# Output weights prepared during the convolution, an in-place norm chain in PSUM, and dt steps spread over the u stage

## The chip, the cores and the metric

The kernel runs on one core of a Trainium2 chip. The metric is the device time of one execution in microseconds, taken as the median of several runs. Before the change the median of 3 runs is 1924.29 us (1920.41 to 1930.12).

## The reference

A layer of a diffusion backbone: 2048 latent tokens of width 1024, with a prefix of 256 context tokens. The tokens are normalised, modulated by `c`, projected once into five parts, and mixed in two ways: a Fourier group of 512 channels (a 2-D DFT, then a linear map, then a SiLU gate) and a state-space group of 1536 channels in 24 heads (a 3x3 depthwise convolution on x, B and C, a chunked scan in both directions, a gated RMSNorm). Both together go through one output projection of 2048 to 1024, are added to the input, and are normalised.

```python
def token_mixer(h, ...):
    u, zf, zs, xbc, dt_raw = jnp.split(h @ w_in, PROJ_SPLITS, axis=-1)
    four = fourier_mixer(u, zf, w_fourier, b_fourier)      # Re(fft2(u)) @ w_f + b_f, times silu(zf)
    xbc = depthwise_conv_grid(xbc, conv_w, conv_b, rows, cols)
    ssd, h_f, h_b = ssd_mixer(xbc, dt_raw, zs, dt_bias, a_log, d_skip, ssd_norm_w, h0_f, h0_b)
    return jnp.concatenate([four, ssd], axis=-1), h_f, h_b
...
    gated = y.reshape(bsz, length, g, r * p) * jax.nn.silu(zs.astype(f32)).reshape(bsz, length, g, r * p)
    gated = gated * lax.rsqrt(jnp.mean(gated * gated, axis=-1, keepdims=True) + EPS)
    out = gated.reshape(bsz, length, D_SSD).astype(zs.dtype) * norm_w
...
    x = x + gate[:, None] * (x_mix @ w_out[i])
return rmsnorm(x, final_norm_w)
```

## The kernel before

All large products are made of three matmuls. An fp32 operand is held as two parts of type fp32r, a high part (a copy with rounding) and a low part (the difference), and the product is high × high + high × low + low × high. `split` makes the parts: ACT copies (line 68), and DVE or POOL subtracts (line 72). Every DMA, load or store, goes through `load` (line 62) on one queue, that of SP; so it stands in one order with all others. A tile framework sets the semaphores and the order of instructions on each engine from the order of the code, from the buffers of each pool (a tile with `bufs=1` must be let go before the next one of its tag may be written), and from `tc.issue_after`, which puts a piece of code behind a given instruction.

The stages, by their time in the profiled execution:

- 0 to about 117 us: modulation, normalisation of x and context, the first projections (dt, parts of zf). The dt rows go to DRAM as `dtT_d`.
- about 117 to 267 us, the **u stage**: a loop over n2 from 0 to 15 (lines 502 to 525). Each step runs 24 matmuls (lines 509 to 511) for 128 tokens, splits the result into `uh` and `ul`, and, one step later, does the first DFT (`u_dft`, line 491), which is stored to `g_d`. Between these steps the dt work of the scan is put in, for three groups of six chunks: `dt_load` (after the steps 2, 6, 10) fetches 96x768 values in two DMAs into `ev` tiles, of which there are two buffers in all; `dt_soft` (steps 3, 7, 11) transposes them on PE (line 433) and computes the softplus in a chain on DVE and ACT (lines 435 to 447, 288 columns wide); `dt_cum` (5, 9, 13) makes the cumulative sums on PE (line 455) and exponentials; `dt_rows` (6, 10, 14) transposes the results back (line 480), splits them into `ev` tiles and stores them to `cum_d` and `q_d`. The steps are in the table `dt_work` (line 490). `ctx_block` at step 2 projects the context for dt and others.
- 267 to about 820 us, the **convolution**: 20 tiles of 128 channels (`conv_tile`). A tile loads its weights into a raw tile with one buffer, splits them, and projects in four blocks of 24 matmuls each into one of two PSUM banks (`pj`); ACT copies each block into an image `img`, which frees the bank. DVE then adds nine taps (`pacc`, line 624), ACT applies SiLU, PE transposes. B and C tiles are split into `sh` and `sl` (one buffer each, `hl_tiles`, line 580) and stored. `gate_step` (line 549) loads one piece of the modulation weights into an `ev` tile after each of the first 16 tiles.
- 820 to about 1130 us: zs projections and the backward scan.
- about 1130 to 1265 us, the **Fourier stage**: tables and second step, then `f_mm(dt, h, i)` (line 961) for four column blocks dt in the order 0, 3, 1, 2, two halves h and two parts i. `zf_load(dt)` (line 895) fetches the gate of a block (1 MB, two buffers), `f_gate` (line 944) multiplies on DVE and POOL, and after a block's second half the result is stored to `fm_d` (line 978). These pieces and the last zs projections are interleaved by given costs.
- 1265 to 1926 us, the **output loop**: 64 units u, of 16 chunks times 4 head groups, in a pipeline of steps s1 to s6 over successive units. `s1` loads decay rows (`rt`, `lt`, `cb`, `chl`) and makes the mask matrix `w` (matmul line 1081 into `parg`, DVE line 1083, ACT, DVE line 1086); `s2` loads, splits the state and runs `pyo` (line 1119); `s3` updates the state; `s4` computes y (`py`, lines 1155 and 1158), gates it (DVE line 1161) and sums its squares; `s5` makes the norm: a matmul with ones into `pn` (line 1171, a PSUM tile with one buffer), Ln, Exp and Square on ACT, then three DVE steps at lines 1177, 1178 and 1180, and the split of the normalised `gt` into `mh` and `ml`; `s6` multiplies by the output weights (lines 1214 to 1216).

The output weights are 16 blocks k of 128x1024 in fp32. Blocks of the state-space group are scaled by the norm weight `ssdw`. They live as high and low parts in `hl` and `hh`, the places of the activations, which become free late. `out_weights` (line 845) loads a block into a raw tile `wo` and splits it: for a scaled block ACT scales (line 858) and DVE scales and subtracts (line 859), for the four others ACT copies and POOL subtracts. Four blocks make the group of a head group g. Group 0 is done just before the rest of the Fourier stage's interleaved pieces; groups 1 to 3 (`out_group`, line 840) follow in the units 1 to 3 of the output loop, each block in two pieces.

Of the kernel before, what the change touches and what calls it, by code (L numbers as in the profile page):

```python
# [49 lines left out]
def mixer_layer(ctx: ExitStack, tc: tile.TileContext, A: dict, out: bass.AP, taps=None):  # L50
# [304 lines left out]
    with ExitStack() as pu:  # L355
# [62 lines left out]
        def dt_load(i):  # L418
            for q0 in range(0, NH, 4):
                nq = min(4, NH - q0)  # L420
                dtTs.append(evac_tile()[:2 * W2, :nq * P])
                load(dtTs[-1], dtT_d[:, (NH * i + q0) * P:(NH * i + q0 + nq) * P])

        def dt_soft(i):
# [4 lines left out]
            for q0 in range(0, NH, 4):  # L429
                nq = min(4, NH - q0)  # L430
                dtT = dtTs.pop(0)
                for q in range(nq):
                    mm(dview(pt)[:, :, q0 + q], dtT[:, q * P:(q + 1) * P], D0["i2"], start=True, stop=True)
# [56 lines left out]
        dt_work = {3 + 4 * i + q: (fn, i) for i in range(3) for q, fn in ((0, dt_soft), (2, dt_cum), (3, dt_rows))}  # L490
# [11 lines left out]
        for n2 in range(16):  # L502
            if n2 == 2:
                ctx_block()
            po = main_psum()
            for k in range(KT):
                a = hh[:, k].rearrange("p (a b) -> p b a", b=16)[:, n2]
                b = hl[:, k].rearrange("p (a b) -> p b a", b=16)[:, n2]
                mm(po, a, wuh[:, k], start=(k == 0), stop=False)
# [20 lines left out]
    gate = gatep.tile([P, D], F32, name="gate")  # L530

    with ExitStack() as pc_:
# [73 lines left out]

        cso = {}
# [81 lines left out]
    ssdw = const_tile("ssdw", hfp)  # L689
# [148 lines left out]
    wcols = [1536, 512, 0, 1024]  # L838

    def out_group(g):  # L840
        with tc.issue_after(fo["st"]), tc.issue_after(units[g]["ld"]), tc.issue_after(units[g]["exp"]):
            for n in range(4 * g, 4 * g + 4):
                out_weights(n, lambda sh: wk.tile(sh, F32, name="wo", tag="xr"), 2)

    def out_weights(n, raw_tile, parts):
        k = worder[n]
        r, c = 2 * (n % 4), wcols[n // 4]
        wos[k] = tuple(t[:, r:r + 2, c:c + 512] for t in (hl, hh))
        for q in range(parts):
            m = 2 // parts  # L850
            hi, lo = (t[:, m * q:m * q + m] for t in wos[k])
            raw = raw_tile([P, m, 512])
            load(raw, A["wout"][k].rearrange("p (a b) -> p a b", a=2)[:, m * q:m * q + m])
            if k < 4:
                split(hi, lo, raw, nc.gpsimd)
            else:
                sc_ = ssdw[:, k - 4:k - 3]
                nc.scalar.activation(hi, raw, AF.Copy, scale=sc_)  # L858
                nc.vector.scalar_tensor_tensor(out=lo, in0=raw, scalar=sc_, in1=hi.bitcast(F32),  # L859
                                               op0=ALU.mult, op1=ALU.subtract)  # L860
# [180 lines left out]
    for n in range(4):  # L1041
        out_weights(n, lambda sh: W["p"].tile(sh, F32, name="wo", tag="raw", bufs=1), 1)
# [6 lines left out]
    for n in range(4, 4):  # L1049
        out_weights(n, lambda sh: W["p"].tile(sh, F32, name="wo", tag="raw", bufs=1), 1)  # L1050
# [117 lines left out]
    def s5(u):  # L1168
# [8 lines left out]
        nc.vector.scalar_tensor_tensor(out=tt, in0=pn, scalar=EPS * GW, in1=tt, op0=ALU.add, op1=ALU.mult)  # L1177
        nc.vector.scalar_tensor_tensor(out=rs, in0=tt, scalar=1.5, in1=rs, op0=ALU.subtract, op1=ALU.mult)
        mx = d["gt"]
        nc.vector.tensor_tensor(out=mx, in0=mx, in1=rs[:].unsqueeze(1).broadcast_to([P, 3, P]), op=ALU.mult)  # L1180
# [71 lines left out]
    for u in range(NU + 2):  # L1252
# [4 lines left out]
        if 0 < u < G:  # L1257
            out_group(u)
# [117 lines left out]
```

## Time and profile before

| | before |
|---|---|
| median of 3 runs | 1924.29 us |
| the profiled execution's own time | 1927.71 us |
| span of the profiled execution | 1925.9 us |
| PE busy | 1824.7 us |
| DVE busy | 1325.2 us |
| ACT busy | 854.5 us |
| POOL busy | 887.0 us |
| DMA, bytes moved | 268.22 MB |

The profile shows one execution. PE, DVE, ACT and POOL are the matrix, vector, activation and general engines, and SPq is the queue of SyncE, which issues the DMAs. "Busy" counts the time of an engine's instructions; PEclk is the clock granted to PE, 1.00 or tenths at full speed. A windows row gives start and end, length, busy time and count of each engine, then PEclk, the mean busy share of the DMA engines and what they moved. A row of a group shows line, engine, operation, output<-inputs, shapes, count, busy time in us, mean ns of one, then the idle time of the engine before these instructions and what ended it. A row of the waits says which engine, tile and line waited for which other, for how long in total, how often and how long at most. A row of the timeline gives start and length in us, and in brackets the idle time before it. A row with three durations gives the least, the median and the greatest in ns, then the first and the last start in us.

### The profile page before, as it was taken

The page shows a single profiled execution, that of the slowest core. Times are in us where ns is not written, and L with a number is a line of the kernel's source. Part 1 is how long each engine was busy: PE and PEld are TensorE (multiplying, and loading weights), DVE is VectorE, ACT ScalarE, POOL GpSimd, SP SyncE. Part 2 cuts the span into 40 slices and gives each one's busy share as a digit, 9 for nine tenths or more (in the row PEclk, how much of TensorE's full clock was granted, in tenths as well). Part 3 has the DMA queues.
Part 4 walks back from the last instruction along what each step waited for, and adds up shares of the span by engine and source line. Part 5 has one row for each costly group of instructions (what it writes and reads, how often), then busy time and mean ns, then how long its engine had stood idle before and what let it go on. Part 6 is the DMA issues. An engine that isn't in the chain of part 4 may idle for free.

```text
span 1925.9 us, 27805 instructions
## 1 busy us (share of the span) xinstructions
PE 1824.7 (95%) x9142; PEld 1501.7 (78%) x9142; DVE 1325.2 (69%) x1830; ACT 854.5 (44%) x1940; POOL 887.0 (46%) x766
## 2 busy tenths in 40 slices
PE   6998899999999999989999999978999999999997
PEld 2787787888888888878888877856777777777775
DVE  3744359888888888748666631478786887688874
ACT  3632114444345344336666653435443444344442
POOL 1321012213123022059777732267766776677742
PEclk9998899999999999999999999979999999999998
DMA  7332243323233233367777774656443444444441
GB/s 272 146 97 80 64 121 111 102 82 94 79 100 103 66 91 99 103 203 214 216 211 213 213 252 152 199 176 185 148 148 117 132 136 135 130 130 135 142 137 39
DMA packets 273169, 268.22 MB, mean 139 GB/s; under 512 B 32545, under 2 KB 240801, under 8 KB 272514
## 3 DMA queue, kind: packets, MB, share of 16 engines
q1 hardware_dynamic: 273026, 266.45, 45.8%
q8 instruction: 73, 1.20, 0.3%
q14 instruction: 70, 0.57, 0.1%
HBM read 180.05 MB, written 86.32 MB: 138 GB/s over the span
## 4 chain that ended last, share of the span: by engine, by line
PE 69%; DVE 6%; DMA 5%; issue 2%; POOL 2%; ACT 1%; SPq 0%; DVEq 0%; ACTq 0%; POOLq 0%
PE pj L177 12%; PE pj L176 12%; PE pj L175 12%; PE po L1216 5%; PE po L1214 5%; PE po L1215 5%; PE py L1155 2%; PE ptr L569 2%; PE parg L1081 2%; PE py L1158 1%; DMA wo<-in_wout 1%; DMA xg<-xtok_d 1%; DVE pacc L624 1%; PE ptr L599 1%; PE ptr L808 1%
## 5 line engine op out<-in xcount | busy, mean ns | idle before, releaser
L177 PE MATMUL pj<-hh,wl 128*128 128x512 f32 x1152 | 452.3, 393 | 1.0 <-POOL wl L72 1.0
L624 DVE SCALAR_TENSOR_TENSOR pacc<-img,c_convw,pacc 128x1024 f32<-128x1024 f32 x320 | 409.8, 1287 | 61.0 <-ACT pacc L621 52.4
L175 PE MATMUL pj<-hh,wh 128*128 128x512 f32 x1152 | 449.3, 394 | 2.5 <-ACT img L68 2.5
L176 PE MATMUL pj<-hl,wh 128*128 128x512 f32 x1152 | 451.5, 392 | 0.0
L72 POOL TENSOR_TENSOR wl<-raw,wh 128x1024 fp32r<-128x1024 f32 x48 | 115.9, 2416 | 476.4 <-ACT wh L68 470.9
L177 PEld LDWEIGHTS pj<-hh,wl 128*128 128x128 f32 x1152 | 216.3, 188 | 47.3 <-POOL wl L72 1.6
L175 PEld LDWEIGHTS pj<-hh,wh 128*128 128x128 f32 x1152 | 216.7, 188 | 43.4 <-ACT img L68 2.7
L176 PEld LDWEIGHTS pj<-hl,wh 128*128 128x128 f32 x1152 | 216.4, 188 | 40.9 <-issue 1.8
L1214 PE MATMUL po<-hl,mh 128*128 128x512 f32 x384 | 158.2, 412 | 2.8 <-ACT hl L858 1.7
L1215 PE MATMUL po<-hh,mh 128*128 128x512 f32 x384 | 154.9, 403 | 1.4 <-DVE hh L859 1.4
L1216 PE MATMUL po<-hl,ml 128*128 128x512 f32 x384 | 149.4, 407 | 5.7 <-POOL ml L72 5.6
L794 ACT ACTIVATE xd<-xt,smb 128x64 f32<-128x64 f32 x384 | 100.8, 336 | 81.4 <-POOL yb L798 79.5
L68 ACT ACTIVATE img<-pj 128x512 f32<-128x512 f32 x80 | 47.6, 594 | 152.7 <-PE pj L177 152.7
L1085 ACT ACTIVATE w<-parg 128x384 f32<-128x384 f32 x128 | 62.2, 486 | 109.7 <-DVE parg L1083 109.4
L72 DVE TENSOR_TENSOR xl<-xw,xh 128x384 fp32r<-128x384 f32 x76 | 65.2, 862 | 55.0 <-ACT xh L68 54.0
L1081 PE MATMUL parg<-rt,lt 128*128 128x384 f32 x256 | 89.7, 376 | 7.5 <-DVE parg L1083 6.5
L1083 DVE COPY_PREDICATED parg<-msk,parg 128x384 f32<-128x384 uint8 x128 | 70.8, 553 | 35.5 <-PE parg L1081 35.2
L1124 POOL TENSOR_TENSOR ts<-ts,yb 128x384 f32<-128x384 f32 x64 | 72.3, 1130 | 48.9 <-issue 25.0
L72 POOL TENSOR_TENSOR ml<-gt,mh 128x384 fp32r<-128x384 f32 x64 | 69.9, 1092 | 54.0 <-ACT mh L68 49.2
L1086 DVE TENSOR_TENSOR w<-w,cb 128x768 f32<-128x768 f32 x64 | 84.6, 1322 | 14.6 <-ACT w L1085 13.8
L68 ACT ACTIVATE xh<-xw 128x384 fp32r<-128x384 f32 x136 | 69.7, 515 | 49.1 <-POOL xw L1135 22.0
L72 DVE TENSOR_TENSOR sl<-hbk,sh 128x384 fp32r<-128x384 f32 x64 | 64.3, 1005 | 37.3 <-ACT sh L68 37.1
(377 smaller groups left out, 4057.5 us busy)
## 6 DMA issues: line engine op xcount, KB each, us to landing
raw<-in_win SPq DMA_DIRECT2D x48, 512.0 KB
xt<-xtok_d SPq DMA_DIRECT2D x80, 192.0 KB
xtok_d<-tk SPq DMA_DIRECT2D x48, 256.0 KB
zsT_d<-ev SPq DMA_DIRECT2D x48, 256.0 KB
yb_d<-yb SPq DMA_DIRECT2D x64, 192.0 KB
yb<-yb_d SPq DMA_DIRECT2D x64, 192.0 KB
zs<-zsT_d SPq DMA_DIRECT2D x64, 192.0 KB
xg<-xtok_d SPq DMA_DIRECT2D x64, 192.0 KB
```

The source lines that it names most:

```text
L68: return nc.scalar.activation(dst, src, AF.Copy).ins
L72: (lo_engine or nc.vector).tensor_tensor(out=lo, in0=src, in1=hi.bitcast(F32), op=ALU.subtract)
L175: mm(po, wh[:, k], a, start=(k == 0), stop=False)
L176: mm(po, wh[:, k], b, start=False, stop=False)
L177: done["mm"] = mm(po, wl[:, k], a, start=False, stop=(k == KT - 1)).ins
L624: nc.vector.scalar_tensor_tensor(out=acc, in0=im[:, r0 + dy:r0 + dy + 16, dx:dx + GRID_W], scalar=tap(t), in1=acc, op0=ALU.mult, op1=ALU.add)
L794: nc.scalar.activation(xd[:, h], d["x"][:, h], AF.Copy, scale=smb[:, 3, c, g * HG + h:g * HG + h + 1])
L1081: mm(po, l[:, dr], r[:, cols], start=True, stop=True)
L1086: nc.vector.tensor_tensor(out=w, in0=w, in1=cb[:].unsqueeze(1).broadcast_to([P, HG, P]), op=ALU.mult)
L1214: mm(po, a, wh[:, i], start=(g == 0 and q == 0), stop=False)
L1215: mm(po, a, wl[:, i], start=False, stop=False)
L1216: mm(po, b, wh[:, i], start=False, stop=(g == 3 and q == 3))
```

## The change

**Output weights.** A new DRAM scratch `wo_d` holds all 16 blocks as high and low parts. After each of the 20 convolution tiles one or two of 32 pieces are made (`wout_piece`): load of 128x512 into an `ev` tile, for the 12 scaled blocks ACT scales it in place, ACT copies it to `sh`, POOL subtracts into `sl`, and both are stored to `wo_d`. `out_weights` and `out_group` are gone; `w_load` only fetches both parts of a block, 512 KB each, into places of `hl` and `hh` that are given by the table `wplace`. Group 0 is fetched before the rest of the Fourier pieces, group 1 among these pieces ahead of the last two pairs of `f_mm`, groups 2 and 3 in the first two steps of the output loop, behind the last store to `fm_d` and the loads of the next unit. The `f_mm` order within the last two blocks becomes (1,0), (2,0), (1,1), (2,1), so that places in `hl` come free sooner.

**dt steps.** A group's dt rows are loaded by one DMA into the raw weight tile instead of two `ev` tiles, after the steps 1, 4 and 9. Softplus runs in steps 2, 7, 12, sums in 5, 10, 14, rows in 6, 11, 15. `ctx_block` moves to step 1.

**Norm chain.** The results of lines 1177 and 1178 are written to `pn` in PSUM in place, and line 1180 reads it there.

```diff
+        def wout_piece(n):
+            k, h = divmod(n, 2)
+            cs = slice(512 * h, 512 * h + 512)
+            raw = evac_tile()
+            load(raw, A["wout"][k][:, cs])
+            if k >= 4:
+                nc.scalar.activation(raw, raw, AF.Copy, scale=ssdw[:, k - 4:k - 3])
+            parts = [t[:].rearrange("p a b -> p (a b)") for t in hl_tiles()]
+            split(*parts, raw, nc.gpsimd)
+            for i in range(2):
+                store(wo_d[k, :, i, cs].bitcast(F32), parts[i].bitcast(F32))
...
             if n < 2 * KT:
                 gate_step(*divmod(n, KT))
+            for q in range(32 * n // 20, 32 * (n + 1) // 20):
+                wout_piece(q)
...
-            for q0 in range(0, NH, 4):
-                nq = min(4, NH - q0)
-                dtTs.append(evac_tile()[:2 * W2, :nq * P])
-                load(dtTs[-1], dtT_d[:, (NH * i + q0) * P:(NH * i + q0 + nq) * P])
+            raw = W["p"].tile([P, 2, 512], F32, name="rawu", tag="raw", bufs=1)
+            dtTs.append(raw[:].rearrange("p a b -> p (a b)")[:2 * W2, :NH * P])
+            load(dtTs[-1], dtT_d[:, NH * P * i:NH * P * (i + 1)])
...
-        dt_work = {3 + 4 * i + q: (fn, i) for i in range(3) for q, fn in ((0, dt_soft), (2, dt_cum), (3, dt_rows))}
+        dt_work = {2 + 5 * i + q: (fn, i) for i in range(3) for q, fn in ((0, dt_soft), (3, dt_cum), (4, dt_rows))}
+        dt_work[14], dt_work[15] = (dt_cum, 2), (dt_rows, 2)
...
-            if n2 in (2, 6, 10):
+            if n2 in (1, 4, 9):
                 dt_load(n2 // 4)
...
+    wplace = [((hl, 1536), (hh, 1536)), ((hl, 0), (hl, 1024)), ((hl, 512), (hh, 1024)), ((hh, 0), (hh, 512))]
+
+    def w_load(n):
+        r, k = 2 * (n % 4), worder[n]
+        wos[k] = tuple(t[:, r:r + 2, c:c + 512] for t, c in wplace[n // 4])
+        for i in range(2):
+            load(wos[k][i].bitcast(F32), wo_d[k, :, i].rearrange("p (a b) -> p a b", a=2).bitcast(F32))
...
+    fmm = [(dt, h) for dt in dts[:2] for h in range(2)] + [(dt, h) for h in range(2) for dt in dts[2:]]
+    for n, (dt, h) in enumerate(fmm):
+        if n in (4, 5):
             side.append((0.0, zf_load(dt)))
+        if n == 6:
+            side.append((0.0, lambda: w_group(1)))
+        side += [(2.6, f_mm(dt, h, i)) for i in range(2)]
...
-        nc.vector.scalar_tensor_tensor(out=tt, in0=pn, scalar=EPS * GW, in1=tt, op0=ALU.add, op1=ALU.mult)
-        nc.vector.scalar_tensor_tensor(out=rs, in0=tt, scalar=1.5, in1=rs, op0=ALU.subtract, op1=ALU.mult)
+        nc.vector.scalar_tensor_tensor(out=pn, in0=pn, scalar=EPS * GW, in1=tt, op0=ALU.add, op1=ALU.mult)
+        nc.vector.scalar_tensor_tensor(out=pn, in0=pn, scalar=1.5, in1=rs, op0=ALU.subtract, op1=ALU.mult)
         mx = d["gt"]
-        nc.vector.tensor_tensor(out=mx, in0=mx, in1=rs[:].unsqueeze(1).broadcast_to([P, 3, P]), op=ALU.mult)
+        nc.vector.tensor_tensor(out=mx, in0=mx, in1=pn[:].unsqueeze(1).broadcast_to([P, 3, P]), op=ALU.mult)
...
-        if 0 < u < G:
-            out_group(u)
+        if u < 2:
+            with tc.issue_after(fo["st"]), tc.issue_after(units[u + 1]["ld"]):
+                w_group(u + 2)
```

The order of SP's DMAs in the u stage, before, around the load for the second dt group (`cum_d` and `q_d` are the stores of the row step before it, `g_d` those of the DFT):

```order
L63 DMA cum_d<-ev 48x512 x2
L63 DMA g_d<-gs 128x4x128
L63 DMA cum_d<-ev 48x256 x2
L63 DMA q_d<-ev 48x512 x2
L63 DMA q_d<-ev 48x256 x2
L63 DMA ev<-dtT_d 96x512
L63 DMA g_d<-gs 128x4x128
L63 DMA ev<-dtT_d 96x256
```

And now, where the loads for the first two groups stand (`rawv` is the context's raw tile, `smb_d` a store of the first sums):

```order
L63 DMA rawv<-in_ctx 128x1024
L63 DMA rawu<-dtT_d 96x768
L63 DMA g_d<-gs 128x4x128
L63 DMA rawu<-dtT_d 96x768
L63 DMA g_d<-gs 128x4x128
L63 DMA dtT_d<-ev 96x256
L63 DMA g_d<-gs 128x4x128
L63 DMA smb_d<-wl 128x144
```

The second group's load stood behind the stores of the first group's rows; it now stands ahead of the first group's sums.

The order of SP's DMAs at the end of the Fourier stage, before (`wo<-in_wout` is a block of group 0, `chl`, `lt` and `rt` are loads of the first units):

```order
L63 DMA zsT_d<-ev 128x4x128
L63 DMA fm_d<-zf 128x16x128
L63 DMA wo<-in_wout 128x1024
L63 DMA zf<-zfT_d 128x2048
L63 DMA fm_d<-zf 128x16x128 x2
L63 DMA chl<-chl_d 128x256 x2
L63 DMA lt_11007<-q_d 6x128
L63 DMA rt_11005<-cum_d 2x6x128
```

And now (the first row is group 1, the pairs after `fm_d` are group 2):

```order
L63 DMA hl<-wo_d 128x2x512 x8
L63 DMA zf<-zfT_d 128x2048
L63 DMA fm_d<-zf 128x16x128 x2
L63 DMA hl<-wo_d 128x2x512
L63 DMA hh<-wo_d 128x2x512
L63 DMA hl<-wo_d 128x2x512
L63 DMA hh<-wo_d 128x2x512
L63 DMA hl<-wo_d 128x2x512
L63 DMA hh<-wo_d 128x2x512
L63 DMA hl<-wo_d 128x2x512
L63 DMA hh<-wo_d 128x2x512
L63 DMA rt_11280<-cum_d 2x6x128
```

Eight loads of 512 KB now stand ahead of the last load of zf, and eight more between the last store of `fm_d` and the third unit's first load.

The order on ACT in the first convolution tile, before (`img` is the image that frees a PSUM bank, `wh` the weights' high part):

```order
L68 ACTIVATE ev<-pj 48x512
L68 ACTIVATE wh<-raw 128x1024
L68 ACTIVATE ev<-pj 48x512
L68 ACTIVATE uh<-pj 128x512
L68 ACTIVATE img_2048<-pj 128x8x64 x2
L621 ACTIVATE pacc<-img_2048,c_convw 128x1024
```

And now:

```order
L68 ACTIVATE ev<-pj 48x512
L68 ACTIVATE wh<-raw 128x1024
L68 ACTIVATE ev<-pj 48x512
L68 ACTIVATE sh<-ev 128x512
L68 ACTIVATE img_2045<-pj 128x8x64 x2
L633 ACTIVATE pacc<-img_2045,c_convw 128x1024
```

The first piece's copy into `sh` now stands ahead of the first two copies into `img`.

More of the change, by code (lines that the diff above doesn't have):

```diff
@@ L92, in mixer_layer @@
     yb_d = scratch("yb_d", [NCH, P, DS])
+    wo_d = scratch("wo_d", [16, P, 2, D], F32R)
     fm_d = scratch("fm_d", [NCH, P, 4, P])
@@ L428, in dt_soft @@
             pt = dt_psum()
[L429 to L433, printed above, removed]
+            dtT = dtTs.pop()
+            for q in range(NH):
+                mm(dview(pt)[:, :, q], dtT[:, q * P:(q + 1) * P], D0["i2"], start=True, stop=True)
             v, e, u, s1_, dtt = (D0[t] for t in ("v", "e", "u", "s1", "dtt"))
@@ L502, in mixer_layer @@
         for n2 in range(16):
-            if n2 == 2:
+            if n2 == 1:
                 ctx_block()
@@ L530, in mixer_layer @@
     gate = gatep.tile([P, D], F32, name="gate")
+    ssdw = const_tile("ssdw", gatep)
     with ExitStack() as pc_:
@@ L688, in mixer_layer @@
     hf = hfp.tile([P, DS], F32, name="hf")
-    ssdw = const_tile("ssdw", hfp)
     pp_ = ctx.enter_context(ExitStack())
@@ L837, in mixer_layer, with w_group @@
     worder = [k for g in range(G) for k in (4 + 3 * g, 5 + 3 * g, 6 + 3 * g, g)]
[L838 to L860, printed above, removed]
+    wplace = [((hl, 1536), (hh, 1536)), ((hl, 0), (hl, 1024)), ((hl, 512), (hh, 1024)), ((hh, 0), (hh, 512))]
[4 more added lines that the diff above has]
+            load(wos[k][i].bitcast(F32), wo_d[k, :, i].rearrange("p (a b) -> p a b", a=2).bitcast(F32))
+    def w_group(g):
+        for n in range(4 * g, 4 * g + 4):
+            w_load(n)
     pfb = ctx.enter_context(ExitStack())
@@ L1015, in mixer_layer @@
     side.append((0.0, f_switch))
-    tail = []
-    for n, dt in enumerate(dts):
-        if n > 1:
+    fmm = [(dt, h) for dt in dts[:2] for h in range(2)] + [(dt, h) for h in range(2) for dt in dts[2:]]
+    for n, (dt, h) in enumerate(fmm):
+        if n in (4, 5):
             side.append((0.0, zf_load(dt)))
-        for h in range(2):
-            for i in range(2):
-                (tail if 2 * n + h >= 8 else side).append((2.6, f_mm(dt, h, i)))
+        if n == 6:
+            side.append((0.0, lambda: w_group(1)))
+        side += [(2.6, f_mm(dt, h, i)) for i in range(2)]
     left = interleave(zs_ops([(i, (3,)) for i in range(19, 7, -1)]), side, 10, .75)
@@ L1039, in mixer_layer @@
         nc.vector.tensor_copy(out=t, in_=st2[:, :2])
-    for n in range(4):
-        out_weights(n, lambda sh: W["p"].tile(sh, F32, name="wo", tag="raw", bufs=1), 1)
+    w_group(0)
     for _, fn in left:
@@ L1048, in mixer_layer @@
     pre2 = preload(LNEXP)
-    for n in range(4, 4):
-        out_weights(n, lambda sh: W["p"].tile(sh, F32, name="wo", tag="raw", bufs=1), 1)
     units = {}
@@ L1090, in mixer_layer @@
         s1(u)
-        for _, fn in tail[len(tail) // 2 * u:len(tail) // 2 * (u + 1)]:
-            fn()
     pfb.close()
```

## The prediction

> **What bounds the kernel now.** I read the page first, then the windows by stage, then PE's waits, then groups and timeline rows. The page:
>
> ```profile
> span 1925.9 us, 27805 instructions
> PE 1824.7 (95%) x9142; PEld 1501.7 (78%) x9142; DVE 1325.2 (69%) x1830; ACT 854.5 (44%) x1940; POOL 887.0 (46%) x766
> PE   6998899999999999989999999978999999999997
> PEclk9998899999999999999999999979999999999998
> ```
>
> PE is busy 95% of the span; time can only come out of its idle slices and of slices where the clock dips. Apart from the two ends, they are slices 4 and 5 (the u stage) and 27 and 28 (start of the output loop), and the change touches both. The windows, in us:
>
> ```profile
> core 0: us, PE busy (x) PEld busy (x) DVE busy (x) ACT busy (x) POOL busy (x), PEclk, DMA share, GB/s
> 0.00:50.00 50.00, 31.78 (x137) 13.73 (x138) 16.67 (x37) 15.81 (x31) 7.96 (x8) 1.00 0.78 278
> 150.00:160.00 10.00, 7.35 (x28) 6.21 (x28) 1.39 (x3) 1.32 (x2) 3.07 (x2) 0.83 0.54 160
> 170.00:180.00 10.00, 7.34 (x21) 6.20 (x22) 4.55 (x11) 1.68 (x4) 0.00 (x0) 0.66 0.35 78
> 190.00:200.00 10.00, 5.04 (x18) 4.12 (x17) 1.61 (x3) 0.86 (x2) 0.00 (x0) 0.78 0.29 80
> 200.00:210.00 10.00, 10.00 (x41) 9.24 (x41) 5.13 (x9) 1.49 (x3) 0.00 (x0) 0.88 0.09 26
> 230.00:240.00 10.00, 7.55 (x31) 6.88 (x32) 0.93 (x3) 0.00 (x0) 0.00 (x0) 0.83 0.22 59
> 267.00:820.00 553.00, 550.49 (x2810) 467.85 (x2809) 463.80 (x390) 235.43 (x361) 115.65 (x74) 1.00 0.33 95
> 1265.00:1360.00 95.00, 72.92 (x353) 54.03 (x352) 75.43 (x114) 48.69 (x107) 71.31 (x66) 0.84 0.60 183
> 1400.00:1880.00 480.00, 460.05 (x2525) 367.45 (x2524) 373.72 (x631) 211.38 (x543) 335.91 (x309) 0.99 0.44 134
> ```
>
> The convolution (267:820) has 2.5 us of idle PE: nothing to win there, only to lose. The steady output loop (1400:1880) has 480 − 460.05 = 20 us idle in 480. Its first 95 us run 353 matmuls, where the steady rate of 2525 / 480 = 5.26 per us would need 67 us: some 28 us are lost.
>
> **Part 1, the dt steps in the u stage.** PE's waits between 117 and 267 us (total, times, longest), and five rows of the timeline, the last two the start and end of a softplus chain on DVE:
>
> ```profile
> PE pj L433 <- DMA ev<-dtT_d: 11.6, 3, 5.0
> PE pj L455 <- DVE wh L447: 5.1, 2, 3.2
> ```
>
> ```profile
> 153.43 1.09 PE L433 MATMUL pj<-wh,ev 96*128 96x48 f32 x8 [2.21 <-DMA ev<-dtT_d]
> 192.96 0.30 SPq L63 DMA_DIRECT2D ev<-dtT_d  x1
> 195.69 1.91 PE L433 MATMUL pj<-wh,ev 96*128 96x48 f32 x8 [4.96 <-DMA ev<-dtT_d]
> 203.61 0.46 DVE L435 TENSOR_TENSOR wh<-pj,wh 128x288 f32<-128x288 f32 x1 [10.23 <-PE pj L433]
> 211.98 0.46 DVE L447 TENSOR_TENSOR wh<-wl,wh 128x288 f32<-128x288 f32 x1
> ```
>
> The load for the second softplus leaves only at 192.96, because its `ev` buffers are held by the stores of the row step in front of it; its first matmul starts at 195.69 after 4.96 us of idle PE. Afterwards the load has a tile of its own and leaves three steps of n2 ahead of its use for the second and third group (n2 4 for 7, 9 for 12), and no store of a row step holds its buffer. A step is 24 matmuls, about 6 us (200:210 ran 41 in 10 us), so 18 us of lead stand against 2.7 us from issue to first use: those waits go. For the first group the distance is still one step (n2 1 for 2), so its 2.21 us stay. The cumulative sums wait 5.1 us for the softplus chain on DVE; they move from two steps behind it to three (two for the third group), and the chain takes 212.44 − 203.61 = 8.8 us, less than two steps once nothing holds up its start: gone. Idle removed: 11.6 + 5.1 − 2.2 = 14.5 us. The clock: behind each gap the windows grant less than 1; (1 − clock) × 10 us is 1.7, 3.4, 2.2, 1.2 and 1.7 in the five windows. The first stays, the others make 8.5, of which I strike 0.5 for half clock on an idle PE. **Part 1: −22.5 us**; bounds −14 (the clock dips anyway) and −26 (the first wait goes too, with its dip).
>
> **Part 2, the output weights split during the convolution.** Added there: 32 pieces of 128x512, after each of 20 convolution tiles one or two. Each is one load and two stores of 256 KB, for 24 of them a scaling on ACT, for all a copy on ACT and a subtraction on POOL. Prices from rows of the same shape:
>
> ```profile
> L858 ACT ACTIVATE hl<-wo,c_ssdw 128x512 fp32r<-128x512 f32 x18 | 12.9, 719 | 9.5 <-DMA wo<-in_wout 9.3
> L68 ACT ACTIVATE sh<-so 128x512 fp32r<-128x512 f32 x16 | 10.1, 633 | 7.7 <-DMA chl_d<-sh 6.9
> L72 POOL TENSOR_TENSOR sl<-so,sh 128x512 fp32r<-128x512 f32 x16 | 20.7, 1296 | 59.3 <-ACT sh L68 39.5 <-DMA chl_d<-sl 19.8
> PE pj L175 <- ACT img L68: 2.5, 1, 2.5
> ```
>
> ACT: 24 × 0.719 + 32 × 0.633 = 37.5 us onto 235 of 553. POOL: 32 × 1.296 = 41.5 onto 116. DMA: 96 transfers, 25.2 MB onto 95 GB/s × 553 us = 52.5 MB, to some 140 GB/s, half of the 278 that 0:50 shows at a share of 0.78. PE stays the bound, so the work itself costs nothing. What can cost is ACT's order: the copy into `sh` waits for the piece's load and for the stores out of the single `sh`, and behind it on ACT stand the copies into `img` that free PE's two PSUM banks. A block is 24 matmuls, again about 6 us, so ACT may stand still some 5 us before PE stops. In the row of sh<-so above 6.9 us of ACT's idle time ended on a store out of `sh` over 16 copies, 0.4 us each; and one such stop shows on PE, of 2.5 us. Two such stops: **+5 us**, bounds 0 and +10 (four). Below 0 nothing, since only 2.5 us are idle there.
>
> **Part 3, the start of the output loop.** Removed from 1217 to 1349 us are 28 loads of `wo` and their splits:
>
> ```profile
> L63 SPq DMA_DIRECT2D wo<-in_wout x28: 332/356/528, 1217.4 to 1349.0; - x28
> L858 ACT ACTIVATE hl<-wo,c_ssdw x21: 706/722/1155, 1230.6 to 1346.6; 128x512 fp32r<-128x512 f32 x18, 128x1024 fp32r<-128x1024 f32 x3
> L859 DVE SCALAR_TENSOR_TENSOR hh<-wo,c_ssdw,hl x21: 741/1023/1566, 1232.2 to 1347.4; 128x512 fp32r<-128x512 f32 x18, 128x1024 fp32r<-128x1024 f32 x3
> PE py L1155 <- DVE w L1086: 5.9, 5, 2.0
> PE pyo L1119 <- DMA chl<-chl_d: 4.4, 4, 3.4
> PE pyo L1119 <- DVE yy L950: 3.2, 1, 3.2
> PE po L1214 <- ACT hl L858: 1.7, 1, 1.7
> PE po L1215 <- DVE hh L859: 1.4, 3, 0.6
> ```
>
> DVE loses 21 × about 1.06 = 22 us and ACT 21 × about 0.78 = 16. The last five rows are PE's largest waits there: only 1.7 + 1.4 us are for the split itself, 9.1 for DVE (`w`, `yy`) and 4.4 for a load. A lighter DVE could win those 9.1, the direct 3.1, and the dips behind them: (1 − 0.84) × 95 = 15 us are lost to the clock. So at best about −15, taking half of the 28.
>
> Against it stand the bytes. A group of weights is now 4 × 2 loads of 512 KB, 4.19 MB, twice what it was. At 278 / 0.78 = 356 GB/s a group takes 11.8 us on all DMA engines. SP issues the eight of group 1 behind fm_d of dt 3, and only then the load of zf for dt 2 and the last two fm_d; then eight of group 2, then the second unit's small loads, and group 3 behind those. Two rows on the zf of dt 2 now:
>
> ```profile
> 1253.54 0.33 SPq L63 DMA_DIRECT2D zf<-zfT_d  x1
> 1261.16 9.95 SPq L63 DMA_DIRECT2D fm_d<-zf  x2
> ```
>
> Were it 11.8 us later, the gates of dt 1 and 2 on DVE and POOL, and the first pyo behind them on PE, begin about 11 us later. Unit 2's loads come another 11.8 us behind group 2, of which the backlog of 18 of the first 24 output matmuls that PE runs ahead of unit 2 (about 4 us) and the late gates cover a part; group 3 comes half under cover. So three groups are 35 us of queue on the way, of which I leave 12 to 13 uncovered, against −15 of work gone: **−2 us**, bounds −15 (the queue is hidden) and +15 (most of it shows).
>
> [...]
>
> **Part 4, the norm chain in place in PSUM.**
>
> ```profile
> L1180 DVE TENSOR_TENSOR gt<-gt,rs 128x384 f32<-128x384 f32 x64 | 53.6, 838 | 1.2
> L1178 DVE SCALAR_TENSOR_TENSOR rs<-tt,rs 128x128 f32<-128x128 f32 x64 | 32.1, 502 | 1.4
> L1177 DVE SCALAR_TENSOR_TENSOR tt<-pn,tt 128x128 f32<-128x128 f32 x64 | 18.2, 285 | 21.4 <-ACT tt L1176 20.9
> L1161 DVE SCALAR_TENSOR_TENSOR gt<-py,zs 128x384 f32<-128x384 f32 x64 | 35.3, 551 | 26.0 <-PE py L1158 14.1 <-POOL xw L1135 5.7 <-issue 3.4
> ```
>
> L1177 reads one operand from PSUM and takes 285 ns where L1178 with the same size reads two from SBUF and takes 502; L1161 with one operand in PSUM takes 551 where L1180 with both in SBUF takes 838. Afterwards L1178 and L1180 each have an operand in PSUM: 64 × (502 − 285) = 13.9 and 64 × (838 − 551) = 18.4, together 32.3 us of DVE, 0.5 us a unit. PE is idle 20 of 480 us in the steady loop, some for DVE; I take a quarter of that, **−5 us**; bounds −15 and +4, since the one `pn` bank is now held until L1180 instead of L1177, and the next unit's norm matmul may wait for it.
>
> [...]
>
> **The sum.** −22.5 + 5 − 2 − 5 = −24.5 us on the profiled execution's 1927.7 us (its span and 1.8 around it), which is 3.4 above the median of 1924.3. The median comes to 1899.8, so **1900**.
>
> **The rivals.**
> (a) *The queue shows at the start of the output loop*: part 3 at +10 to +15 and the rest as forecast: 1912 to 1917, about 1915. For it: eight half-megabyte loads stand in front of zf and of unit 2. Against it: PE has other work queued, and the DMA share there is 0.60. Chance 0.20.
> (b) *Everything comes in*: part 3 at −15, part 4 at −10, part 2 at 0: about 1877, between 1868 and 1888. For it: DVE and ACT lose 38 us exactly where PE waits for DVE. Chance 0.15.
> (c) *The dt change doesn't do what it says*: the chain on DVE stays as long, PE now reaches the sums sooner, and waits of the same size move to them; part 1 gives −4 instead of −22.5: 1918. For it: DVE began 203.61 − 195.69 = 8 us after the first matmul of its step. Against it: the added step of distance. Chance 0.10.
> (d) *Slower*: ACT stops at the pieces. A piece's copy sits on ACT until its load has come and the stores of the piece before have left `sh`; if that keeps the `img` copies back by 1.5 us beyond PE's two banks in each of 32 pieces, part 2 costs 48 and the time is 1900 + 43 = 1943. It decides where ACT stands more than 5 us at a time; the 6.9 us in 16 copies speak against it, the doubled traffic for it. Part 2 must reach 39 of those 48 us to bring the time past 1933.9. Chance 0.10.
> The forecast itself, 1888 to 1912, has 0.45.
>
> **How the numbers follow.** 0.5%, or 9.6 us, is about what a measurement of this kernel can tell from no change: faster means under 1914.7, slower over 1933.9. Faster: forecast 0.45, (b) 0.15, half of (a) 0.10: 0.70, less 0.02 for its tails, 0.68. Same: the other half of (a) 0.10, (c) 0.10: 0.20. Slower: (d) and the tails, 0.12. The range runs from inside (b), 1874, through (a) and (c) to 1926, the sum with parts 2 and 3 at their dear ends (1922) and a little; it leaves out (d) and the low part of (b).
>
> **What would show it.** Part 1: PE's wait for the dt load 2 us instead of 11.6, that for L447 under 1, and a clock of 1.0 in all windows of the u stage but one or two. Part 2: PE idle under 13 us from 267 to 820, with `img` on ACT named as releaser. Part 3: the first units' norm matmuls come within a few us of where they were, counted from the end of the convolution; PE's waits name loads rather than DVE. Part 4: L1178 near 285 ns, L1180 near 550. I am wrong if the convolution is longer by over 10 us, if L1180 stays at 838, or if the first 95 us of the output loop lose more than 45.

## The result, and the profile after

| | before | after |
|---|---|---|
| median of 5 runs | 1924.29 us | 1913.20 us |
| the profiled execution's own time | 1927.71 us | 1912.61 us |
| its span | 1925.9 us | 1910.8 us |

The changed kernel takes 0.9937 of the time before, with a 95% interval of 0.9915 to 0.9958: 11.1 us less in the medians, 15.1 in the two spans. The prediction was 1900 us, a gain of 24.3. Faster was right, the size was less than half. The page after:

```profile
span 1910.8 us, 28132 instructions
PE 1809.4 (95%) x9142; PEld 1492.4 (78%) x9142; DVE 1258.5 (66%) x1809; ACT 873.9 (46%) x1968; POOL 906.2 (47%) x791
PE   6989999999999999989999999957999999999997
PEclk8999999999999999999999999977999999999999
```

The hole in slices 4 and 5 is gone. The one in slices 27 and 28 is still there, and deeper (5, where the lowest digit was 7). The same in windows; the start of the output loop, which was 1265 to 1360, now lies at 1250 to 1345:

```profile
core 0: us, PE busy (x) PEld busy (x) DVE busy (x) ACT busy (x) POOL busy (x), PEclk, DMA share, GB/s
150.00:160.00 10.00, 9.77 (x49) 9.36 (x48) 7.03 (x12) 1.87 (x4) 0.12 (x1) 1.00 0.33 93
170.00:180.00 10.00, 10.00 (x52) 9.54 (x52) 3.55 (x8) 2.86 (x6) 0.00 (x0) 1.00 0.34 72
190.00:200.00 10.00, 10.00 (x44) 9.84 (x44) 6.91 (x13) 1.80 (x4) 0.00 (x0) 1.00 0.30 86
200.00:210.00 10.00, 10.00 (x46) 9.67 (x45) 4.05 (x8) 2.38 (x5) 0.00 (x0) 1.00 0.18 43
230.00:240.00 10.00, 10.00 (x45) 9.78 (x45) 6.93 (x13) 2.35 (x5) 1.07 (x1) 1.00 0.46 130
245.00:795.00 550.00, 544.51 (x2773) 460.39 (x2772) 462.74 (x391) 268.43 (x416) 162.80 (x109) 1.00 0.45 140
1250.00:1345.00 95.00, 59.19 (x281) 46.11 (x280) 43.55 (x76) 26.55 (x63) 46.99 (x46) 0.75 0.73 238
1400.00:1880.00 480.00, 465.49 (x2590) 373.23 (x2589) 349.51 (x640) 215.15 (x548) 331.01 (x313) 1.00 0.44 133
```

DVE and ACT have less to do there (43.6 and 26.6 us, from 75.4 and 48.7), partly because fewer units get through: PE does 281 matmuls in 95 us, where it did 353.

A table by stage puts every kernel on one scale. Each number is the distance between two rows of the timeline in that kernel's profiled execution: the first matmul of the u stage, the first of the convolution, the end of the last SiLU of a convolution tile, the start of the last three Fourier matmuls, the norm matmul of unit 8, that of unit 63. "Scan and Fourier" joins everything from that SiLU to those matmuls. In the first three columns, kernels with the same code in a stage differ by up to 4 us or so. In the last two they differ by more, because the mark at unit 8 can move by 7 us while the sum of the two columns hardly changes; a table behind the experiments has that sum.

| us in the stage | u stage | convolution | scan and Fourier | output start, to unit 8 | units 8 to 63 |
|---|---|---|---|---|---|
| before | 149.9 | 542.6 | 454.2 | 114.9 | 527.0 |
| after | 126.2 | 549.6 | 454.9 | 125.2 | 515.8 |
| difference | −23.7 | +7.0 | +0.7 | +10.3 | −11.2 |
| forecast | −22.5 | +5 | 0 | −2 | −5, over all units |

Together −16.9; the rest of the 15.1 is 1.7 us in front of the u stage. Three terms are near their forecast or better, one is wrong in sign: the start of the output loop. These are PE's largest waits there (total, times, longest; `issue` names no other engine):

```profile
PE pyo L1115 <- DVE yy L951: 16.5, 1, 16.5
PE parg L1079 <- DMA rt<-cum_d: 4.1, 1, 4.1
PE pyo L1115 <- DMA chl<-chl_d: 3.6, 3, 1.9
PE pn L1167 <- DVE s L1161: 3.1, 2, 1.9
PE py L1151 <- issue: 2.9, 1, 2.9
PE parg L1079 <- DMA lt<-q_d: 2.1, 1, 2.1
```

The waits for `hl` and `hh` have gone, that for `w` fell from 5.9 us to 1.3, and one of 16.5 us has come. It is put down to DVE's `yy`, but the timeline of SP's queue shows what is behind `yy`:

```profile
1239.65 0.37 SPq L63 DMA_DIRECT2D fm_d<-zf  x1
1240.97 8.29 SPq L63 DMA_DIRECT2D hl<-wo_d  x8
1249.31 1.23 SPq L63 DMA_DIRECT2D zf<-zfT_d  x1
1266.04 2.84 SPq L63 DMA_DIRECT2D fm_d<-zf  x2
```

```profile
1267.32 0.66 PE L1115 MATMUL pyo<-sh,chl 128*128 128x384 f32 x1 [16.47 <-DVE yy L951]
```

The eight loads of group 1 are issued from 1240.97 on, the last zf behind them at 1249.31; the gates that need it are stored at 1266.04, and PE stands until 1267.32. For a part of that time the queue itself stands still, since the next entries in it are the two stores of `fm_d`, which wait for the gates:

```profile
1262.00:1266.00 4.00, 0.00 (x0) 0.00 (x0) 3.41 (x6) 0.60 (x1) 3.11 (x3) 0.50 0.00 0
```

### The profile page after: what moved, and what is told of

The parts are those of the page before. It is cut to its first block, busy times and chain, and to the rows that moved or that the text cites. A ratio compares the mean times of both kernels' runs of the same rounds, so it can differ in the third digit from the quotient of the medians.

```text
span 1910.8 us, 28132 instructions
## 1 busy us (share of the span) xinstructions
PE 1809.4 (95%) x9142; PEld 1492.4 (78%) x9142; DVE 1258.5 (66%) x1809; ACT 873.9 (46%) x1968; POOL 906.2 (47%) x791
## 4 chain that ended last, share of the span: by engine, by line
PE 75%; DMA 9%; DVE 5%; POOL 5%; issue 3%; ACT 2%; SPq 1%; POOLq 0%; DVEq 0%; ACTq 0%
PE pj L178 11%; PE pj L177 11%; PE pj L176 11%; PE po L1212 6%; PE po L1210 6%; PE po L1211 6%; PE py L1151 2%; PE parg L1079 2%; POOL sl L72 2%; PE pj L508 1%; PE pj L509 1%; PE pj L510 1%; PE py L1154 1%; DMA ev<-in_wout 1%; PE ptr L569 1%
## 5 line engine op out<-in xcount | busy, mean ns | idle before, releaser
L1210 PE MATMUL po<-hl,mh 128*128 128x512 f32 x288 | 117.5, 408 | 0.7 <-ACT mh L68 0.4
L1211 PE MATMUL po<-hh,mh 128*128 128x512 f32 x288 | 114.8, 399 | 0.0
L1212 PE MATMUL po<-hl,ml 128*128 128x512 f32 x288 | 109.8, 401 | 2.6 <-POOL ml L72 2.4
L1120 POOL TENSOR_TENSOR ts<-ts,yb 128x384 f32<-128x384 f32 x64 | 73.6, 1150 | 57.6 <-issue 27.2
L1079 PE MATMUL parg<-rt,lt 128*128 128x384 f32 x256 | 88.0, 372 | 11.2 <-DMA rt<-cum_d 4.1
L1084 DVE TENSOR_TENSOR w<-w,cb 128x768 f32<-128x768 f32 x64 | 81.6, 1275 | 12.1 <-ACT w L1083 10.9
L72 DVE TENSOR_TENSOR sl<-hbk,sh 128x384 fp32r<-128x384 f32 x64 | 59.9, 937 | 38.4 <-ACT sh L68 38.2
L72 POOL TENSOR_TENSOR sl<-ev,sh 128x512 fp32r<-128x512 f32 x32 | 42.1, 1317 | 89.1 <-DMA wo_d<-sl 38.3
```

Source lines behind the costliest of these rows:

```text
L72: (lo_engine or nc.vector).tensor_tensor(out=lo, in0=src, in1=hi.bitcast(F32), op=ALU.subtract)
L1079: mm(po, l[:, dr], r[:, cols], start=True, stop=True)
L1084: nc.vector.tensor_tensor(out=w, in0=w, in1=cb[:].unsqueeze(1).broadcast_to([P, HG, P]), op=ALU.mult)
L1120: nc.gpsimd.tensor_tensor(out=ts, in0=ts, in1=yb, op=ALU.add)
L1210: mm(po, a, wh[:, i], start=(g == 0 and q == 0), stop=False)
L1211: mm(po, a, wl[:, i], start=False, stop=False)
```

## The experiments

Times are medians; ratios are to the kernel before on the same chip, and since the runs were spread over several chips, small differences are better read from the ratios.

**The two small parts alone.** The kernel before with the dt part of the diff and nothing else:

```diff
-            if n2 in (2, 6, 10):
+            if n2 in (1, 4, 9):
                 dt_load(n2 // 4)
...
-        dt_work = {3 + 4 * i + q: (fn, i) for i in range(3) for q, fn in ((0, dt_soft), (2, dt_cum), (3, dt_rows))}
+        dt_work = {2 + 5 * i + q: (fn, i) for i in range(3) for q, fn in ((0, dt_soft), (3, dt_cum), (4, dt_rows))}
+        dt_work[14], dt_work[15] = (dt_cum, 2), (dt_rows, 2)
```

> The kernel before with the dt part alone. Theory (the stage's own account): the u stage, from its first matmul to the first one of the convolution, went from 149.9 to 126.2 us in the changed kernel, all of it through the dt steps; so this kernel is 20 to 25 us faster than before, about 1901, with that stage at 126 to 128 us. Rival (c) of the prediction: part 1 brings only some 4 us in the whole program, 1920, because the time is lost again further on.

Measured: 1905.80 us, 0.9898 (0.9884 to 0.9913), 19.1 less, just short of the 20 to 25 expected. The u stage takes 125.8 us, so the theory holds there and rival (c) is out. But the convolution takes 547.8 instead of 542.6, without a single piece of output weights in it: some 5 us are given back. Then the norm chain alone:

```diff
-        nc.vector.scalar_tensor_tensor(out=tt, in0=pn, scalar=EPS * GW, in1=tt, op0=ALU.add, op1=ALU.mult)
-        nc.vector.scalar_tensor_tensor(out=rs, in0=tt, scalar=1.5, in1=rs, op0=ALU.subtract, op1=ALU.mult)
+        nc.vector.scalar_tensor_tensor(out=pn, in0=pn, scalar=EPS * GW, in1=tt, op0=ALU.add, op1=ALU.mult)
+        nc.vector.scalar_tensor_tensor(out=pn, in0=pn, scalar=1.5, in1=rs, op0=ALU.subtract, op1=ALU.mult)
...
-        nc.vector.tensor_tensor(out=mx, in0=mx, in1=rs[:].unsqueeze(1).broadcast_to([P, 3, P]), op=ALU.mult)
+        nc.vector.tensor_tensor(out=mx, in0=mx, in1=pn[:].unsqueeze(1).broadcast_to([P, 3, P]), op=ALU.mult)
```

> The kernel before with the norm chain in place in PSUM alone. Theory: the 11.2 us won between the norms of unit 8 and unit 63 (527.0 to 515.8 us) are the norm chain's; this kernel is 9 to 14 us faster than before, about 1913, with DVE lighter by some 32 us. Rival: the term of the prediction was right, 5 us, and the rest of the 11.2 came from the weights being out of the way; then about 1919 and 522 us between units 8 and 63.

Measured: 1913.96 us, 0.9943 (0.9928 to 0.9958), 10.9 less, and 515.3 us between the units 8 and 63. The theory holds: the chain alone brings what the changed kernel won in the steady loop, about twice the forecast. Groups of this kernel:

```profile
L1180 DVE TENSOR_TENSOR gt<-gt,pn 128x384 f32<-128x384 f32 x64 | 35.0, 547 | 1.0
L1178 DVE SCALAR_TENSOR_TENSOR pn<-pn,rs 128x128 f32<-128x128 f32 x64 | 18.8, 295 | 1.4
L1177 DVE SCALAR_TENSOR_TENSOR pn<-pn,tt 128x128 f32<-128x128 f32 x64 | 18.7, 292 | 20.7 <-ACT tt L1176 20.6
```

The means of the rows before hide why this works. In the kernel before, L1178 takes 288 ns (276 to 294) in the 21 cases in which no POOL instruction runs beside it, and 659 on average (up to 1150) in the 37 that start while POOL is at work; L1180 takes 555 (544 to 560) in 24 cases without POOL and 1073 (579 to 1541) in the 35 that start while POOL works. Two rows of L1178 in the kernel before, the second with the POOL instruction beside it, then one of the norm chain alone:

```profile
1398.72 0.29 DVE L1178 SCALAR_TENSOR_TENSOR rs<-tt,rs 128x128 f32<-128x128 f32 x1
1437.71 1.01 POOL L1124 TENSOR_TENSOR ts<-ts,yb 128x384 f32<-128x384 f32 x1 [1.12 <-issue]
1438.33 0.54 DVE L1178 SCALAR_TENSOR_TENSOR rs<-tt,rs 128x128 f32<-128x128 f32 x1
```

```profile
1413.00 1.01 POOL L72 TENSOR_TENSOR sl<-hf,sh 128x384 fp32r<-128x384 f32 x1 [0.35 <-ACT sh L68]
1413.48 0.30 DVE L1178 SCALAR_TENSOR_TENSOR pn<-pn,rs 128x128 f32<-128x128 f32 x1
```

The slow one ends at 1438.87, 0.15 us behind the POOL instruction; the one with an operand in PSUM ends at 1413.78, while POOL works until 1414.01. With one operand in PSUM, L1178 and L1180 take 295 and 546 ns when they start beside POOL, the same as without it (296 and 549). So what the change takes away is not a dearer read of SBUF but time in which a DVE instruction with both operands in SBUF is held up while POOL runs. L1086, whose operands both stay in SBUF, shows the same in the kernel before: 958 ns in 8 cases without POOL, 1434 in 49 beside it. No run here moves POOL's work away as a test of its own.

**Without the output weights.** Both edits together on the kernel before, so the changed kernel without its largest part:

> Before with the dt part and the norm chain, without the change of the output weights. Theory: the weights cost the changed kernel 7 us in the convolution and 10 us at the start of the output loop; without them the time is 1913 - 17 = about 1896, so this kernel beats the changed one by 10 to 20 us. Rival: the weights pay for themselves elsewhere, and this kernel is within 5 us of the changed one, 1908 to 1918.

Measured: 1898.36 us, 0.9868 (0.9849 to 0.9886). It is 14.8 us faster than the changed kernel (13 by the two ratios), and the intervals do not touch: the change of the output weights, the greater part of the diff, costs time. By stages, its convolution takes 547.6 us (549.6 with the pieces), and its start of the output loop 108.1 (125.2 with the loads).

**The order in the queue.** The changed kernel with zf's last load put ahead of group 1:

```diff
-            load(zf[:].rearrange("p a b -> p (a b)"), zfT_d[dt])
+            fo["zl"] = load(zf[:].rearrange("p a b -> p (a b)"), zfT_d[dt])
...
         if n == 6:
-            side.append((0.0, lambda: w_group(1)))
+            def g1():
+                with tc.issue_after(fo["zl"]):
+                    w_group(1)
+            side.append((0.0, g1))
```

> The changed kernel with the load of zf for the last column block put ahead of the eight loads of weight group 1, nothing else moved. Theory (the queue, rival (a) of the prediction): PE's one wait of 16.5 us of the first pyo for yy falls to 3 to 5 us, and the time falls by 8 to 13 us to about 1902. Rival: the loads of groups 2 and 3 set the pace of units 2 to 4 anyway, the first pyo comes earlier and the time won is waited for at units 2 and 3; then 1909 to 1913.

Measured: 1910.05 us, 0.9920 (0.9908 to 0.9932), 3 us less than the changed kernel, with intervals that overlap: the rival in time. The wait for `yy` fell by 10 us, as the theory has it, and another grew:

```profile
PE parg L1082 <- DMA rt<-cum_d: 8.1, 1, 8.1
PE pyo L1118 <- DVE yy L951: 6.3, 1, 6.3
PE py L1154 <- DVE w L1087: 4.0, 3, 2.8
```

The start takes 117.1 us, 8 less, but the units 8 to 63 take 520.4 instead of 515.8, so more than half of what was won is lost again there. Then also the groups 2 and 3 one step later:

```diff
-        if u < 2:
-            with tc.issue_after(fo["st"]), tc.issue_after(units[u + 1]["ld"]):
-                w_group(u + 2)
+        if 0 < u < 3:
+            with tc.issue_after(fo["st"]), tc.issue_after(units[u + 1]["ld"]):
+                w_group(u + 1)
```

> The changed kernel with zf's last load ahead of group 1 (as in the run before) and groups 2 and 3 each issued one step later, behind the loads of the third and the fourth unit instead of ahead of them. Theory (order in the queue): unit 2 no longer waits behind 4.2 MB; from the end of the Fourier matmuls to the norm of unit 8 some 108 to 112 us instead of 117 to 125, about 1902. Rival (bytes): 12.6 MB have to pass in these five units whatever the order; each unit only meets another group, and the stretch stays at 116 to 120 us, about 1909.

Measured: 1909.58 us, 0.9929 (0.9902 to 0.9957). The start takes 128.0 us, longer than any and outside both forecasts: unit 4's first matmuls wait where unit 2's did. The units 8 to 63 take 511.3. In time the rival was right, and the theory that these changes of order win 10 us falls. That no order would win it is not shown by two orders.

**Without the loads.** The changed kernel with no loads of the groups 1 to 3:

```diff
-        for i in range(2):
+        for i in range(2 if n < 4 else 0):
```

> The changed kernel with the loads of weight groups 1 to 3 left out (their places keep older data, so the output is not the reference's). Theory: the loads in SP's queue are all that makes the start of the output loop longer, and without them the work taken from DVE and ACT shows: from the end of the Fourier matmuls to the norm of unit 8 about 95 to 100 us instead of 125, near 1886. Rival: taking the splits off DVE and ACT is worth nothing, since PE there waits for other steps; then 107 to 110 us, as in the kernel without the change of the weights, near 1897.

Measured: 1882.86 us, 0.9799 (0.9774 to 0.9823), and 92.5 us for the start: the theory, and a little more. It is 30.3 us faster than the changed kernel (27 by the two ratios). So the two halves of part 3 come apart. Taking the splits off DVE and ACT is worth 108.1 − 92.5 = 15.6 us, and the loads cost 125.2 − 92.5 = 32.7. The windows of the changed kernel show them at work:

```profile
1240.00:1250.00 10.00, 10.00 (x46) 8.29 (x45) 2.23 (x4) 4.37 (x7) 8.00 (x9) 1.00 1.08 335
1250.00:1260.00 10.00, 0.85 (x5) 0.46 (x3) 0.00 (x0) 0.00 (x0) 0.00 (x0) 0.67 1.04 397
1280.00:1290.00 10.00, 7.52 (x29) 5.49 (x25) 2.04 (x5) 2.03 (x5) 1.00 (x1) 0.79 0.86 312
1290.00:1300.00 10.00, 5.50 (x24) 3.94 (x23) 4.78 (x9) 2.66 (x6) 5.39 (x5) 0.55 0.93 310
1300.00:1310.00 10.00, 3.12 (x8) 2.38 (x9) 2.31 (x5) 2.26 (x6) 0.99 (x1) 0.50 0.67 239
```

And the same ten microseconds each of the kernel without the loads:

```profile
1250.00:1260.00 10.00, 3.86 (x18) 2.95 (x16) 4.66 (x8) 0.60 (x1) 4.86 (x6) 0.79 0.32 112
1280.00:1290.00 10.00, 9.65 (x57) 7.88 (x56) 5.31 (x11) 3.91 (x11) 4.33 (x5) 1.00 0.57 172
1290.00:1300.00 10.00, 10.00 (x57) 8.27 (x55) 7.46 (x15) 5.95 (x16) 8.87 (x11) 1.00 0.65 191
1300.00:1310.00 10.00, 10.00 (x63) 8.23 (x59) 6.43 (x12) 4.02 (x11) 6.41 (x7) 1.00 0.41 124
```

Between 1250 and 1260 all four engines stand nearly still in the changed kernel while the DMA engines are full (share 1.04, 397 GB/s): nothing is left to work on, since the zf load stands behind those bytes. Not all of PE's 16.5 us there are the loads', though: without them the first `pyo` still waits 6.2 us for `yy`. Between 1290 and 1310 PE is busy 8.6 us of 20, where it is busy for all 20 without the loads.

**Half the bytes.** To tell bytes from the number of loads and their places, every load of the groups 1 to 3 fetches half its rows:

```diff
-            load(wos[k][i].bitcast(F32), wo_d[k, :, i].rearrange("p (a b) -> p a b", a=2).bitcast(F32))
+            m = 2 if n < 4 else 1
+            load(wos[k][i][:, :m].bitcast(F32), wo_d[k, :, i].rearrange("p (a b) -> p a b", a=2)[:, :m].bitcast(F32))
```

> The changed kernel with the same loads of weight groups 1 to 3 in the same order, each fetching only the first half of its rows, 256 KB instead of 512 (the other half keeps older data, so the output is not the reference's). Without these loads the stretch from the end of the Fourier matmuls to the norm of unit 8 took 92.5 us, with all of them 125.2. Theory (bytes): half the bytes cost half of the 32.7, the stretch is 106 to 112 us, the time about 1897. Rival (places in the queue): what counts is the number of loads in front and the waits for their places to come free, and it stays at 120 to 126 us, about 1912.

Measured: 109.1 us for the start, between 92.5 and 125.2 just where half the bytes should put it (108.9). The time is 1903.62 us, 0.9889 (0.9858 to 0.9921), 9.6 less than the changed kernel instead of the 16 that were expected of the whole; the units 8 to 63 took 522.8 us here, 7 more. Up to unit 8 the theory holds. Over the whole output loop half the bytes win only 9 of the 30 us that all of them cost, as the sums below show, so the rival is not out: the number of loads or their places may carry a part, and these runs don't divide it.

**The 5 us given back.** The kernel with dt part and norm chain, the dt steps set closer together, so that the last rows are done in n2 13:

```diff
-        dt_work = {2 + 5 * i + q: (fn, i) for i in range(3) for q, fn in ((0, dt_soft), (3, dt_cum), (4, dt_rows))}
-        dt_work[14], dt_work[15] = (dt_cum, 2), (dt_rows, 2)
+        dt_work = {2 + 4 * i + q: (fn, i) for i in range(3) for q, fn in ((0, dt_soft), (2, dt_cum), (3, dt_rows))}
...
-            if n2 in (1, 4, 9):
+            if n2 in (1, 4, 8):
```

> The kernel with dt part and norm chain but the old output weights, and the dt steps closer together: softplus in steps 2, 6, 10, sums in 4, 8, 12, rows in 5, 9, 13, loads after 1, 4, 8. In the two runs with the dt part and no pieces in the convolution, the convolution took 548 us instead of 543. Theory: the last row step in n2 15 runs into the first convolution tiles on ACT and gives back those 5 us; here the convolution takes 543 to 545 and the u stage no more than 127, so 3 to 5 us are won, about 1894. Rival: the third step between softplus and sums is what took the 5.1 us of waits for L447 away; then PE waits for it again, 3 to 5 us, and the time stays at about 1898 or above.

Measured: 1887.81 us, 0.9826 (0.9804 to 0.9849), faster than before by 34 us, and than the changed kernel by 21 by the two ratios and 25 by the medians: the best version that computes the reference. The convolution takes 544.0 us and the u stage 127.4, as the theory has it; no wait for the sums came back. PE's waits for `img` in the convolution, first with the long spacing (dt part and norm chain), then here:

```profile
PE pj L175 <- ACT img L68: 5.8, 2, 4.1
```

```profile
PE pj L175 <- ACT img L68: 2.4, 1, 2.4
```

Its lead over the kernel with the long spacing is 10.5 us by the medians, 8 by the two ratios. Of it 3.6 us are from the convolution. The units 8 to 63 took 507.5 us instead of 518.0, but the start of the output loop 115.3 instead of 108.1, so the loop as a whole gives some 3. The two profiled executions lie 6.7 us apart, which the convolution and the loop make up; why the loop got shorter is not explained. And the same spacing in the changed kernel:

> The changed kernel with the dt steps closer together as in the run that did so without the change of the weights (softplus 2, 6, 10, sums 4, 8, 12, rows 5, 9, 13, loads after 1, 4, 8). There the convolution took 544.0 us. Theory: the pieces cost the convolution some 2 us only, as the two kernels with the longer spacing showed (549.6 with, 547.6 without): 545 to 547 us here, and the time falls by 3 to 8 us to about 1907. Rival: the prediction's +5 was right and was only covered by the wait of the row step; then 549 us or more and a time within 3 us of the changed kernel, 1910 to 1916.

Measured: 1904.33 us, 0.9893 (0.9872 to 0.9915). The convolution takes 550.7 us: the theory's 545 to 547 is missed, and the rival's number is met. Without pieces it was 544.0, so alone the pieces cost 6.7 us; next to the late row step they cost 2 (549.6 against 547.6). The two do not add up in PE's waits for ACT either: 5.8 us with the late row step alone, 5.3 with the pieces alone, 5.3 with both. The time did fall by 8.9 us, but not there: from unit 8 to unit 63 it took 508.4 instead of 515.8. PE's waits in this convolution name ACT both times:

```profile
PE ptr L568 <- ACT tk L68: 3.5, 3, 1.7
PE pj L176 <- ACT img L68: 1.8, 1, 1.8
```

**The output loop in all these kernels.** The last two columns of the stage table, and their sum:

| us | start, to unit 8 | units 8 to 63 | together |
|---|---|---|---|
| before | 114.9 | 527.0 | 642 |
| norm chain alone | 109.0 | 515.3 | 624 |
| dt part and norm chain | 108.1 | 518.0 | 626 |
| the same, dt steps closer | 115.3 | 507.5 | 623 |
| changed kernel | 125.2 | 515.8 | 641 |
| zf first | 117.1 | 520.4 | 638 |
| zf first, groups 2 and 3 later | 128.0 | 511.3 | 639 |
| half the bytes | 109.1 | 522.8 | 632 |
| no loads | 92.5 | 518.6 | 611 |
| changed, dt steps closer | 125.5 | 508.4 | 634 |

By the sums the change of the weights costs the output loop 15 us: 30 for the loads, less 15 for the splits that it takes away.

## Why the prediction was wrong, point by point

**Part 1 was right, with a remainder unforeseen.** The stage gave −23.7 for a forecast of −22.5. PE's waits in the changed kernel's u stage:

```profile
PE ptr L242 <- DVE rawv L233: 3.8, 1, 3.8
...
PE pj L431 <- DMA rawu<-dtT_d: 0.2, 1, 0.2
```

The wait for the dt load fell from 11.6 us to 0.2 (even the first one went), that for line 447 from 5.1 to none, and the clock is 1.00 in all five windows. The context block, moved to step 1, brought one new wait of 3.8 us for `rawv`. What the prediction did not have: the row step moved to n2 15 keeps ACT busy into the first convolution tiles, and 3 to 5 us go there (5.2 by the run with the dt part alone, 3.6 by the closer spacing). As a whole the dt part is worth 19.1 us, not 22.5.

**Part 2 was right in size.** Forecast +5; the closer spacing shows +6.7, while in the changed kernel itself the pieces add only about 2 to what the row step costs. Of the 6.7 us, 2.9 are longer waits for ACT (5.3 against 2.4), and most of the 5.3 are for `tk`, not for `img` as forecast; the rest is time in which PE counts as busy, and it is not explained. No wait names POOL or a DMA. Rival (d) did not occur.

**Part 3 failed, at one step:** "three groups are 35 us of queue on the way, of which I leave 12 to 13 uncovered". The 35 us were right and nearly none of them was covered: the runs show 32.7 up to unit 8 and 30 over the loop. The other half of the part, "at best about −15", was right as well (15.6). So the net is +17 against a kernel that keeps the old weights, and +10.3 in the stage table, where the norm chain helps (alone it takes the start from 114.9 to 109.0); −2 was forecast. Why was there no cover? The prediction took the gates and 18 output matmuls for work that would fill PE while the queue runs. But the gates needed zf, and each unit's small loads stand in the same queue: all of PE's work soon depends on something behind the 4.2 MB. The step before it, the price from 278 GB/s at a share of 0.78, was good: group 1 kept the DMA engines at a share of 1.04 to 1.08. The average share of 0.60, which the prediction took as evidence against rival (a), says nothing on such a burst. In the trace zf was issued behind group 1, at 1249.31, and its packets (8 KB each) moved from 1257 to 1261, when all but the last of the group's (2 KB each) were through. It was the mechanism of rival (a), 1912 to 1917, that came. That 1913.2 lies in its range is in part luck, since the weights cost the loop 15 to 17 us by themselves, part 1 won less than forecast, and part 4 more.

**Part 4 was right in its durations and too small in its effect.** DVE's three steps went from 53.6 + 32.1 + 18.2 = 103.9 us to 72.5 in the run with the norm chain alone, 31.4 less for 32.3 forecast; the durations are those that were read off the neighbouring rows. The prediction gave no reason for them, and took means over instructions that POOL held up and others that it didn't. Beside POOL's work the saving is large (659 to 295 ns for L1178), without it there is none (288 to 296, and 555 to 549 for L1180).

What was mis-sized is the share that reaches PE: 10.9 us measured, 5 forecast as a quarter of 20 us of idle PE. Idle time was too narrow a base. PE's idle time from 1400 to 1880 fell from 20 to 16 us, about as forecast:

```profile
1400.00:1880.00 480.00, 463.99 (x2566) 371.79 (x2565) 350.46 (x645) 213.79 (x550) 325.45 (x310) 0.99 0.44 133
```

but 2566 matmuls ran in it instead of 2525, and 41 more are some 8 us at 5.26 per us. So time was won inside what counts as busy as well. How, no run here shows. The start of the output loop gave 5.9 us more in this run's profile. (That execution was the fastest of six, so its stages show more than the 10.9 us of the medians.)

**The sum.** In the runs the dt part is worth −19.1, the norm chain −10.9, both together −26.5, and the output weights +13 to +15. The prediction had −22.5, −5 and +3 for the last.

## What to carry to other kernels

A load that takes the place of a computation is not free because the DMA share is low on average: look at the stretch where it falls, divide its bytes by the rate at which the DMA engines are full (here 397 GB/s at a share of 1.04), and ask whether any engine has work that depends on nothing behind it in the queue. If not, expect its whole duration on the path; here it was 30 of 35 us, and two other orders won no more than 3 to 4. When work moves out of a loop, price both halves apart, and try the small parts of a change alone: here the two small ones were worth 26 us, and the large one cost 13 to 15. And where a row of a group has a mean, look at the spread: L1178 and L1180 were fast or slow according to what POOL did beside them, and the mean of 502 ns for L1178 was the duration of neither.

## What was not expected

- Moving a step within the u stage changed the output loop, whose code is the same. With the old weights the start grew by 7.2 us and the units 8 to 63 shrank by 10.5; in the changed kernel the start stayed and they shrank by 7.4. The two kernels with norm chain and old weights differ in the order of PE's instructions in more than a hundred places, about two thirds of them in the last two fifths of the program: the framework's ordering carries a shift to the end. Whether that order makes the difference was not tried, and so 7 of the 8.9 us of the last run stay open.
- Between 1250 and 1260, with the loads of group 1 and zf, the DMA engines moved 397 GB/s at a share of 1.04, where 356 had been worked out from the start of the program.
- In the changed kernel's profiled execution the clock dips in the first 50 us (0.83 from 0 to 50, 1.00 before); the u stage begins at 119.0 us (117.3 before), so little came of it.
